# Scores of a sparse-attention step: heads in pairs, the query's high part with the key's low part as two products of 64 rows

## The chip, the cores and the metric

The kernel runs on one core of a Trainium2 chip. The metric is the device time of one execution in microseconds (us), lower is better; the profile and the times below are of the kernel before the change.

## What is computed

One inference step of a decoder of two layers. The first mixes tokens by sparse attention: an indexer scores every key for every query, the best keys are selected, and attention runs over those. The second uses a gated convolution; both have a gated MLP. There are 1024 new prompt tokens and 8 x 4 sample tokens. Cut to the parts that the change touches:

```python
def indexer_scores(qi, wi, ki):
    s = jnp.einsum('bqhd,bsd->bqhs', qi, ki, preferred_element_type=jnp.float32)
    return jnp.einsum('bqhs,bqh->bqs', jax.nn.relu(s), wi.astype(jnp.float32))
...
    s = jnp.einsum('bqkgd,bqjkd->bqkgj', qg, k_sel, preferred_element_type=jnp.float32) * (HEAD_DIM ** -0.5)
    s = jnp.where(valid[:, :, None, None, :], s, -jnp.inf)
    p = jax.nn.softmax(s, axis=-1).astype(v_sel.dtype)
```

Both have 16 heads of 64 dimensions; in the attention four heads share one key head. Prompt queries are worked on in blocks of 128.

## The kernel before

Every fp32 operand of a product is split into a high part (rounded to the matrix format) and a low part (the rest), and a product is built from the products of these parts. `split` (L125) does this: ScalarE copies the high part, VectorE or GpSimd subtracts.

A head has 64 dimensions and TensorE takes 128 rows, so in the scores both parts of a query stand in one stationary tile: the high part in rows 0 to 63 and the low part in rows 64 to 127. The keys' high part stands twice, in both halves of the rows of one tile, and the keys' low part twice in another. So two products of 128 rows, with the high and then with the low keys, add up all four combinations in one PSUM bank. There are three places:

- `index_tile` (L254) makes the indexer queries of block t: `stacks` (L195) writes both parts of each head side by side and `transposed` (L201) turns them into the tile `QI`. For blocks 2 and 3 it goes on to the scores (L278, L279), a relu on ScalarE (L281) and a weighted sum over the heads on VectorE (L285). Blocks 4 to 7 store `QI`.
- `late_scores` (L290) does the scores of blocks 4 to 7 later (L306 holds both products, then L307 and L311), in chunks of up to 512 columns.
- `attend` (L525) does the attention scores of four heads per key head and block (L553, L554). The tile `Q` holds the high part of all rows from ScalarE (L544); GpSimd then subtracts in rows 64 to 127 (L545). VectorE adds the selection bias and takes the maximum while it reads the bank (L555). Then come the exponential (L561), the division on GpSimd (L564), transposes (L570) and the product with the values (L574).

The banks of these products come from the pool tile `ix`: four of them while the index tiles run, two later. The rows of `late_scores` come from a pool tile `e` with 8 buffers.

The other work on TensorE is three products per weight tile in `product` (L711; L719, L720, L722) for the projections behind the attention, the convolution and the MLP, and the input projections (L172 to L174). Scores, selection and attention run as background: generators that `weave` advances between pieces of the foreground, each `yield` with the cost that it stands for. That sets the order in which the program is written; a scheduler that simulates a timeline then sets each engine's own order, and each engine works through its queue in that order.

The sample tokens have products with few rows elsewhere: L629 and L630 (32 rows), L360 (64) and the transposes L689 (64 rows, 64 columns); the change leaves them as they are.

Of the kernel before, what the change touches and what calls it, by code (L numbers as in the profile page):

```python
# [4 lines left out]
F32 = mybir.dt.float32  # L5
# [4 lines left out]
AF = mybir.ActivationFunctionType  # L10
OP = mybir.AluOpType
# [5 lines left out]
NEG = -1e30  # L17
# [54 lines left out]
RL = 4  # L72
R2, D0 = 0.5, 0
F0, R0, R1, C1, C2 = 14, 0.8, 1.0, 115, 70
class Net:
# [119 lines left out]
    def stacks(self, x, rows, n):  # L195

        s = self.p1.tile([128, 16, 128], F32R, name="sq", bufs=1)
        self.split(s[:rows, :n, 0:64], s[:rows, :n, 64:128], x, pool=True)
        return s

    def transposed(self, out, s, n):  # L201
# [52 lines left out]
    def index_tile(self, t, w, q=None):  # L254
        nc = self.nc
        rows = 128 if t < 8 else 32
        if q is None:
            q = self.project(t, w)
        pk = self.new_keys(t, q, q[:rows, 0:WI0].rearrange("p (h d) -> p h d", d=64))
        wi = self.wi[t] if t in self.wi else self.p1.tile([128, 16], F32, name="wi", bufs=2)  # L260
        nc.vector.tensor_scalar(wi[:rows], q[:rows, WI0:WIDX], 1.0 / 32.0, None, op0=OP.mult)
        if t == 8:
            self.index_sample(q, wi, pk)
            return
        s = self.stacks(q[:, 0:1024].rearrange("p (h d) -> p h d", d=64), 128, 16)
        QI = self.p1.tile([128, 16, 128], F32R, name="QI", bufs=2)
        self.transposed(QI, s, 16)
        if t > 3:
            nc.sync.dma_start(self.dQI[t - 4], QI.bitcast(F32))
            self.weave(13.0)  # L270
            return
        n = 128 * (t + 1)
        sc = self.sc[t]
        for h in range(16):
            for c in range(0, n, 512):
                m = min(512, n - c)
                p = self.psx.tile([128, 512], F32, name="ix", bufs=self.nix)[:, :m]
                nc.tensor.matmul(p, QI[:, h, :], self.KIh[:, c:c + m], start=True, stop=False)  # L278
                nc.tensor.matmul(p, QI[:, h, :], self.KIl[:, c:c + m], start=False, stop=True)  # L279
                r = self.p1.tile([128, 512], F32, name="rl", bufs=RL)[:, :m]  # L280
                nc.scalar.activation(r, p, AF.Relu)  # L281
                if h == 0:
                    nc.vector.tensor_scalar(sc[:, c:c + m], r, wi[:, 0:1], None, op0=OP.mult)
                else:
                    nc.vector.scalar_tensor_tensor(sc[:, c:c + m], r, wi[:, h:h + 1], sc[:, c:c + m],  # L285
                                                   op0=OP.mult, op1=OP.add)
            self.weave(n / 512.0)
        nc.vector.tensor_add(sc[:, n - 128:n], sc[:, n - 128:n], self.tri)

    def late_scores(self, blocks, T, K):  # L290

        nc = self.nc
        for t in blocks:
            n = 128 * (t + 1)
            sc = self.sc[t] = T("e", [128, 1024], F32)[:, :n]
            wi = self.wi[t]
            for h in range(16):
                if h % 8 == 0:
                    Q = T("e", [128, 8, 128], F32R)
                    nc.sync.dma_start(Q.bitcast(F32), self.dQI[t - 4][:, h:h + 8])  # L300
                r = T("e", [128, 1024], F32)[:, :n]
                for c in range(0, n, 512):
                    m = min(512, n - c)
                    p = self.psx.tile([128, 512], F32, name="ix", bufs=self.nix)[:, :m]
                    for z in range(2):
                        nc.tensor.matmul(p, Q[:, h % 8, :], K[z][:, c:c + m], start=(z == 0), stop=(z == 1))  # L306
                    nc.scalar.activation(r[:, c:c + m], p, AF.Relu)  # L307
                if h == 0:
                    nc.vector.tensor_scalar(sc, r, wi[:, 0:1], None, op0=OP.mult)
                else:  # L310
                    nc.vector.scalar_tensor_tensor(sc, r, wi[:, h:h + 1], sc, op0=OP.mult, op1=OP.add)  # L311
                yield n / 960.0 + 0.15
            nc.vector.tensor_add(sc[:, n - 128:n], sc[:, n - 128:n], self.trib)

    def index_sample(self, q, wi, pk):
# [209 lines left out]
    def attend(self, g, T, blocks, vs=range(4)):  # L525

        nc = self.nc
        N = 128 * (max(blocks) + 1)
        for v in vs:
            kr = T("r", [128, N], F32)  # L530
            KH, KL = T("KH", [128, N], F32R), T("KL", [128, N], F32R)
            for z in range(2):
                nc.sync.dma_start(kr[64 * z:64 * z + 64], self.dK[v // 2, 64 * (v % 2):64 * (v % 2) + 64, 0:N])
            self.split(KH, KL, kr, pool=True)
            vr = T("qr", [128, N // 128, 64], F32)
            V = T("V", [128, N // 128, 128], F32R)
            nc.sync.dma_start(vr, self.dV[v, :, 0:N // 128])
            self.split(V[:, :, 0:64], V[:, :, 64:128], vr, pool=True)
            for i in blocks:
                n = 128 * (i + 1)  # L540
                qr, Q = T("qr", [128, 4, 128], F32), T("Q", [128, 4, 128], F32R)
                for z in range(2):
                    nc.sync.dma_start(qr[64 * z:64 * z + 64], self.dQ[i][:, 4 * v:4 * v + 4])
                nc.scalar.activation(Q, qr, AF.Copy)  # L544
                nc.gpsimd.tensor_sub(Q[64:128], qr[64:128], Q[64:128].bitcast(F32))  # L545
                st = self.pf.tile([128, 4, 4], F32, name="ast", bufs=2)
                es = []
                for j in range(4):
                    e = T("e", [128, N], F32)
                    for z, c in enumerate(range(0, n, 512)):  # L550
                        m = min(512, n - c)
                        p = self.psx.tile([128, 512], F32, name="ix", bufs=self.nix)[:, :m]
                        nc.tensor.matmul(p, Q[:, j], KH[:, c:c + m], start=True, stop=False)  # L553
                        nc.tensor.matmul(p, Q[:, j], KL[:, c:c + m], start=False, stop=True)  # L554
                        nc.vector.tensor_tensor_reduce(  # L555
                            e[:, c:c + m], p, self.bias[i][:, c:c + m], scale=1.0, scalar=NEG, op0=OP.add,
                            op1=OP.max, accum_out=st[:, j, z:z + 1])
                    if n > 512:
                        nc.vector.tensor_max(st[:, j, 0:1], st[:, j, 0:1], st[:, j, 1:2])
                    nc.vector.tensor_scalar(st[:, j, 1:2], st[:, j, 0:1], -0.125, None, op0=OP.mult)  # L560
                    nc.scalar.activation(e[:, :n], e[:, :n], AF.Exp, bias=st[:, j, 1:2], scale=0.125,  # L561
                                         accum_out=st[:, j, 2:3])
                    nc.vector.reciprocal(st[:, j, 3:4], st[:, j, 2:3])  # L563
                    nc.gpsimd.tensor_scalar(e[:, :n], e[:, :n], st[:, j, 3:4], 1.0, op0=OP.mult, op1=OP.mult)  # L564
                    es.append(e)
                o = self.psv.tile([128, 512], F32, name="pv", bufs=NPV)
                for c in range(i + 1):
                    p = self.tr()
                    for j in range(4):
                        nc.tensor.transpose(p[:, 128 * j:128 * j + 128], es[j][:, 128 * c:128 * c + 128], self.ident)  # L570
                    pp = T("pp", [128, 2, 512], F32R)
                    self.split(pp[:, 0], pp[:, 1], p)
                    for z in range(2):
                        nc.tensor.matmul(o, V[:, c], pp[:, z], start=(c == 0 and z == 0), stop=(c == i and z == 1))  # L574
                ot = T("ot", [64, 512], F32)
                nc.scalar.activation(ot, o[64:128], AF.Copy)
                u = T("ou", [128, 2, 128], F32)
                pick = lambda x, par: x.rearrange("p (c e q) -> p e c q", e=2, q=128)[:, par]
                for par in range(2):
                    nc.vector.tensor_add(u[64 * par:64 * par + 64], pick(ot, par), pick(o[0:64], par))  # L580
                c = g.cols(i)
                nc.sync.dma_start(self.do[g.name][:, 2 * v:2 * v + 2, c:c + 128], u)
                yield n / 100.0 + 2.0
# [874 lines left out]
```

## Time and profile before

| what | value |
|---|---|
| median of 3 runs | 2837.78 us (2833.9 to 2841.37) |
| profiled execution, its own time | 2835.95 us |
| its span | 2834.1 us |
| mean granted TensorE clock | 0.971 of 2.4 GHz |
| TensorE busy | 96% of the span, 15999 products |
| VectorE, ScalarE, GpSimd busy | 64%, 46%, 24% |
| chain of waits by engine | TensorE 74%, VectorE 11%, ScalarE 5%, issue 4%, DMA 4%, GpSimd 2% |

How to read it: a row's busy time is a sum over the whole span, while the kernel has stages with different limits; the index tiles run from some 59 us, the first attention from 250, the late scores from 404 to 684, the second attention from 684 to 1020 and from 1143 to 1340 us with the sample tokens between, and from 1500 us on there are weight products alone. The chain of waits is followed back from the last instruction: at each step to what released it, or to the instruction before it on its engine. Ends of products on TensorE are modelled and overlap the next product; their starts are measured, so the step from start to start is the price of a product in a stream.

### The profile page before, as it was taken

The page shows a single profiled execution, that of the slowest core. Times are in us where ns is not written, and L with a number is a line of the kernel's source. Part 1 is how long each engine was busy: PE and PEld are TensorE (multiplying, and loading weights), DVE is VectorE, ACT ScalarE, POOL GpSimd, SP SyncE. Part 2 cuts the span into 40 slices and gives each one's busy share as a digit, 9 for nine tenths or more (in the row PEclk, how much of TensorE's full clock was granted, in tenths as well). Part 3 has the DMA queues.
Part 4 walks back from the last instruction along what each step waited for, and adds up shares of the span by engine and source line. Part 5 has one row for each costly group of instructions (what it writes and reads, how often), then busy time and mean ns, then how long its engine had stood idle before and what let it go on. Part 6 is the DMA issues. An engine that isn't in the chain of part 4 may idle for free.

```text
span 2834.1 us, 43012 instructions
## 1 busy us (share of the span) xinstructions
PE 2707.1 (96%) x15999; PEld 2379.6 (84%) x15999; DVE 1813.9 (64%) x3348; ACT 1317.1 (46%) x2263; POOL 693.1 (24%) x1026
## 2 busy tenths in 40 slices
PE   7989989899999989997999999999999999999997
PEld 7878757688777868875888999999789987999996
DVE  4474566998889855677686454445754566754446
ACT  4574674765886553356353332323422234432323
POOL 4364641211122354124350000001300031200001
PEclk8989999799999979999999999999999999999999
DMA  4145435133233324331523332323332322332332
GB/s 142 37 165 140 139 104 161 45 90 98 70 91 88 93 82 134 103 91 32 151 78 93 90 90 90 86 80 115 88 91 72 101 80 74 120 90 86 90 92 73
DMA packets 141713, 271.50 MB, mean 96 GB/s; under 512 B 27457, under 2 KB 68865, under 8 KB 140865
## 3 DMA queue, kind: packets, MB, share of 16 engines
q1 hardware_dynamic: 138816, 259.32, 30.8%
q0 software_dynamic: 2688, 9.44, 1.1%
q8 instruction: 126, 2.06, 0.3%
q14 instruction: 83, 0.67, 0.1%
HBM read 245.34 MB, written 23.36 MB: 95 GB/s over the span
## 4 chain that ended last, share of the span: by engine, by line
PE 74%; DVE 11%; ACT 5%; issue 4%; DMA 4%; POOL 2%; SPq 0%; DVEq 0%; ACTq 0%; POOLq 0%
PE mm L722 16%; PE mm L719 16%; PE mm L720 16%; PE m L719 4%; PE m L722 4%; PE m L720 4%; PE pj L172 2%; PE pj L174 2%; PE pj L173 2%; DVE wl L129 2%; PE pv L574 1%; ACT tkb L409 1%; DVE pp L129 1%; PE ix L306 1%; PE tr L570 1%
## 5 line engine op out<-in xcount | busy, mean ns | idle before, releaser
L128 ACT ACTIVATE wh<-raw 128x1024 fp32r<-128x1024 f32 (+2 forms) x456 | 384.3, 843 | 785.4 <-PE mm L720 620.0
L129 DVE TENSOR_TENSOR wl<-raw,wh 128x1024 fp32r<-128x1024 f32 (+2 forms) x456 | 468.1, 1027 | 290.7 <-ACT wh L128 286.3
L719 PE MATMUL mm<-xhB,wh 128*128 128x272 f32 x1920 | 518.4, 289 | 0.0
L720 PE MATMUL mm<-xlB,wh 128*128 128x272 f32 x1920 | 516.6, 287 | 0.0
L722 PE MATMUL mm<-xhB,wl 128*128 128x272 f32 x1920 | 396.6, 288 | 0.6 <-DVE wl L129 0.6
L719 PEld LDWEIGHTS mm<-xhB,wh 128*128 128x128 f32 x1920 | 361.9, 189 | 0.3
L720 PEld LDWEIGHTS mm<-xlB,wh 128*128 128x128 f32 x1920 | 360.8, 188 | 0.3
L722 PEld LDWEIGHTS mm<-xhB,wl 128*128 128x128 f32 x1920 | 299.7, 188 | 0.9 <-DVE wl L129 0.9
L719 PE MATMUL mm<-hh,wh 128*128 128x272 f32 (+1 forms) x992 | 293.7, 311 | 6.0 <-DVE r L760 2.3
L720 PE MATMUL mm<-hl,wh 128*128 128x272 f32 (+1 forms) x992 | 292.5, 310 | 1.9 <-DVE hl L129 1.9
L719 PE MATMUL m<-xhA,wh 128*128 128x512 f32 x608 | 243.0, 401 | 4.9 <-DVE h L844 2.4
L722 PE MATMUL mm<-hh,wl 128*128 128x272 f32 (+1 forms) x992 | 243.9, 311 | 2.2 <-DVE wl L129 2.2
L720 PE MATMUL m<-xlA,wh 128*128 128x512 f32 x608 | 241.6, 397 | 3.0 <-DVE xlA L129 3.0
L722 PE MATMUL m<-xhA,wl 128*128 128x512 f32 x608 | 241.3, 397 | 1.2 <-DVE wl L129 1.0
L719 PEld LDWEIGHTS mm<-hh,wh 128*128 128x128 f32 x992 | 186.5, 188 | 17.9 <-ACT wh L128 4.2
L720 PEld LDWEIGHTS mm<-hl,wh 128*128 128x128 f32 x992 | 186.7, 188 | 11.0 <-DVE hl L129 2.7
L821 POOL COPY ffn_outs<-ext 128x2 f32<-128x2 f32 x44 | 25.8, 586 | 605.9 <-ACT ext L890 605.9
L722 PEld LDWEIGHTS mm<-hh,wl 128*128 128x128 f32 x992 | 161.9, 188 | 12.1 <-DVE wl L129 3.2
L760 DVE TENSOR_TENSOR r<-r,mm 128x544 f32<-128x544 f32 (+1 forms) x128 | 90.5, 708 | 122.6 <-PE mm L722 122.1
L129 DVE TENSOR_TENSOR pp<-tr,pp 128x512 fp32r<-128x512 f32 x168 | 117.7, 713 | 53.6 <-ACT pp L128 53.2
L172 PE MATMUL pj<-W,X 128*128 128x512 f32 (+2 forms) x352 | 133.9, 384 | 16.8 <-ACT W L128 13.3
L564 POOL TENSOR_SCALAR e<-e,ast 128x128 f32<-128x128 f32 (+7 forms) x128 | 101.7, 800 | 194.0 <-DVE ast L563 156.7
(370 smaller groups left out, 5896.8 us busy)
## 6 DMA issues: line engine op xcount, KB each, us to landing
raw<-w_up SPq DMA_DIRECT2D x176, 512.0 KB, 3.5
raw<-w_down SPq DMA_DIRECT2D x128, 256.0 KB, 2.7
raw<-w_ci SPq DMA_DIRECT2D x48, 512.0 KB, 3.6
X<-xp SPq DMA_DIRECT2D x24, 512.0 KB, 3.6
raw<-w_down SPq DMA_DIRECT2D x64, 192.0 KB, 2.4
qr<-dQ SPq DMA_DIRECT2D x64, 128.0 KB, 3.0
raw<-w_ao SPq DMA_DIRECT2D x16, 512.0 KB, 3.5
raw<-w_co SPq DMA_DIRECT2D x32, 256.0 KB, 2.6
```

What stands on the lines that cost most here:

```text
L128: nc.scalar.activation(hi, src, AF.Copy)
L129: (nc.gpsimd if pool else nc.vector).tensor_sub(lo, src, hi.bitcast(F32))
L172: nc.tensor.matmul(p, xh[:, k, :], wh[k][:, s], start=(k == 0), stop=False)
L173: nc.tensor.matmul(p, xh[:, k, :], wl[k][:, s], start=False, stop=False)
L174: nc.tensor.matmul(p, xl[:, k, :], wh[k][:, s], start=False, stop=(k == 7))
L306: nc.tensor.matmul(p, Q[:, h % 8, :], K[z][:, c:c + m], start=(z == 0), stop=(z == 1))
L409: nc.scalar.activation(signs[:r, :n], xs[i], AF.Sign, bias=thr[:r, i:i + 1], scale=-1.0, accum_out=cnt[:r, i:i + 1])
L564: nc.gpsimd.tensor_scalar(e[:, :n], e[:, :n], st[:, j, 3:4], 1.0, op0=OP.mult, op1=OP.mult)
L719: nc.tensor.matmul(o, wh[:, k, :], xh[:, c:c + m], start=(k == 0), stop=False)
L720: nc.tensor.matmul(o, wh[:, k, :], xl[:, c:c + m], start=False, stop=False)
L722: nc.tensor.matmul(o, wl[:, k, :], xh[:, c:c + m], start=False, stop=(k == n - 1))
L760: nc.vector.tensor_add(rv, rv, acc)
```

## The change

The heads are taken in pairs. In the stationary tile the even head keeps its high part in rows 0 to 63, and the odd head has it in rows 64 to 127 (and its low part in rows 0 to 63). The products with the high keys keep 128 rows. The product with the low keys takes the 64 rows of the query's high part alone: rows 0 to 63 for the even head, 64 to 127 for the odd one. The product of both low parts is left out. A new function `qk` issues the four products of a pair: high, high, low, low.

```diff
     def stacks(self, x, rows, n):
         s = self.p1.tile([128, 16, 128], F32R, name="sq", bufs=1)
-        self.split(s[:rows, :n, 0:64], s[:rows, :n, 64:128], x, pool=True)
+        four = s[:rows, :n].rearrange("p (i e) (z d) -> p i (e z) d", e=2, z=2)
+        self.split(four[:, :, 0::3], four[:, :, 1:3], x.rearrange("p (i e) d -> p i e d", e=2), pool=True)
...
+    def qk(self, ps, Q, hi, lo):
+        mm = self.nc.tensor.matmul
+        for p, q in zip(ps, Q):
+            mm(p, q, hi, start=True, stop=False)
+        for z, (p, q) in enumerate(zip(ps, Q)):
+            s = slice(64 * z, 64 * z + 64)
+            mm(p, q[s], lo[s], start=False, stop=True)
...
     def late_scores(self, blocks, T, K):
...
-                r = T("e", [128, 1024], F32)[:, :n]
+                rs = [T("e", [128, 1024], F32)[:, :n] for e in range(2)]
                 for c in range(0, n, 512):
                     m = min(512, n - c)
-                    p = self.psx.tile([128, 512], F32, name="ix", bufs=self.nix)[:, :m]
-                    for z in range(2):
-                        nc.tensor.matmul(p, Q[:, h % 8, :], K[z][:, c:c + m], start=(z == 0), stop=(z == 1))
-                    nc.scalar.activation(r[:, c:c + m], p, AF.Relu)
...
+                    ps = [self.psx.tile([128, 512], F32, name="ix", bufs=self.nix)[:, :m] for e in range(2)]
+                    self.qk(ps, (Q[:, h0 % 8, :], Q[:, h0 % 8 + 1, :]), K[0][:, c:c + m], K[1][:, c:c + m])
+                    for r, p in zip(rs, ps):
+                        nc.scalar.activation(r[:, c:c + m], p, AF.Relu)
...
-                yield n / 960.0 + 0.15
+                yield n / 480.0 + 0.3
...
     def attend(self, g, T, blocks, vs=range(4)):
...
-                nc.gpsimd.tensor_sub(Q[64:128], qr[64:128], Q[64:128].bitcast(F32))
+                for z in range(2):
+                    lo = lambda x: x[64 - 64 * z:128 - 64 * z].rearrange("p (i e) q -> p i e q", e=2)[:, :, z]
+                    nc.gpsimd.tensor_sub(lo(Q), lo(qr), lo(Q).bitcast(F32))
...
-                        nc.tensor.matmul(p, Q[:, j], KH[:, c:c + m], start=True, stop=False)
-                        nc.tensor.matmul(p, Q[:, j], KL[:, c:c + m], start=False, stop=True)
...
+                        self.qk(ps, (Q[:, j], Q[:, j + 1]), KH[:, c:c + m], KL[:, c:c + m])
```

`index_tile` calls `qk` in the same way. In `attend` the pair's two rows are reduced right behind `qk`, and the steps from the maximum on (L558 to L564) are written behind all four heads.

The built program has 352 products of 64 rows (L296 in the changed code; L293 are those with the high keys). Where they stand in TensorE's queue, in the late scores (`ix` the bank, `KH` and `KL` the high and low keys, `e_4835` and `e_4851` the queries), is shown first of before and then of the change:

```order
L306 MATMUL ix_4882<-KH_4446,e_4835 128x512
L306 MATMUL ix_4882<-KL_4447,e_4835 128x512
L306 MATMUL ix_4886<-KH_4446,e_4835 128x256
L306 MATMUL ix_4886<-KL_4447,e_4835 128x256
L306 MATMUL ix_4892<-KH_4446,e_4835 128x512
L306 MATMUL ix_4892<-KL_4447,e_4835 128x512
L306 MATMUL ix_4896<-KH_4446,e_4835 128x256
L306 MATMUL ix_4896<-KL_4447,e_4835 128x256
```

```order
L293 MATMUL ix_4909<-KH_4462,e_4851 128x512
L296 MATMUL ix_4909<-KL_4463,e_4851 128x512
L293 MATMUL ix_4910<-KH_4462,e_4851 128x512
L296 MATMUL ix_4910<-KL_4463,e_4851 128x512
L293 MATMUL ix_4917<-KH_4462,e_4851 128x256
L296 MATMUL ix_4917<-KL_4463,e_4851 128x256
L293 MATMUL ix_4918<-KH_4462,e_4851 128x256
L296 MATMUL ix_4918<-KL_4463,e_4851 128x256
```

The two heads of a chunk now follow each other where a head's two chunks did, but high and low alternate as before: the order high, high, low, low in which `qk` is written isn't kept here. At 28 places it is, as at this one between weight products of the MLP (`m1`), again in the late scores and on TensorE:

```order
L732 MATMUL m1_5080<-xlA_4428,wh_5082 128x512
L293 MATMUL ix_4855<-KH_4462,e_4851 128x512
L293 MATMUL ix_4856<-KH_4462,e_4851 128x512
L296 MATMUL ix_4855<-KL_4463,e_4851 128x512
L296 MATMUL ix_4856<-KL_4463,e_4851 128x512
L734 MATMUL m1_5080<-xhA_4427,wl_5083 128x512
```

Here the two low products stand next to each other. In the second attention, on TensorE between transposes (`tr`) and products with the values (`pv`), they stand apart:

```order
L582 MATMUL tr_11112<-ident_154,e_11014 128x128
L293 MATMUL ix_11288<-KH_11248,Q_11260 128x512
L296 MATMUL ix_11288<-KL_11249,Q_11260 128x512
L586 MATMUL pv_11051<-pp_11107,V_10558 128x512
L293 MATMUL ix_11295<-KH_11248,Q_11260 128x384
L296 MATMUL ix_11295<-KL_11249,Q_11260 128x384
L586 MATMUL pv_11051<-pp_11107,V_10558 128x512
```

A single low product stands between products of 128 rows, as in 296 of the 324 places in all; the place of the scores among the other work has hardly moved.

## Rows read from the trace of the kernel before

**Rows 1.** Busy table of the page: us, share, instructions.

```profile
PE 2707.1 (96%) x15999; PEld 2379.6 (84%) x15999; DVE 1813.9 (64%) x3348; ACT 1317.1 (46%) x2263; POOL 693.1 (24%) x1026
```

**Rows 2.** Windows by stage: stretch, length, busy by engine, granted clock, DMA share, GB/s.

```profile
59.00:146.00 87.00, 85.45 (x497) 72.48 (x496) 44.66 (x54) 52.06 (x104) 27.42 (x31) 1.00 0.12 37
250.00:404.00 154.00, 143.86 (x726) 112.53 (x724) 85.00 (x321) 100.73 (x239) 92.97 (x155) 0.99 0.46 130
404.00:700.00 296.00, 273.81 (x1165) 219.46 (x1166) 251.60 (x433) 179.56 (x324) 50.00 (x73) 0.93 0.31 94
700.00:1020.00 320.00, 302.84 (x1395) 243.60 (x1393) 273.89 (x623) 232.50 (x392) 88.61 (x127) 0.96 0.31 91
1143.00:1340.00 197.00, 181.32 (x861) 142.84 (x860) 141.15 (x361) 103.31 (x176) 60.26 (x57) 0.97 0.27 78
1500.00:2834.00 1334.00, 1307.33 (x9306) 1245.18 (x9304) 738.32 (x1106) 430.44 (x664) 161.41 (x288) 1.00 0.30 90
```

**Rows 3.** Chain of waits by line in 59:146, 404:700, 560:690 and 1143:1340, in turn.

```profile
by line: PE pj L172 15.8%; PE pj L174 15.4%; PE pj L173 15.2%; PE ix L360 9.1%; DVE sc L285 7.6%; PE ix L278 5.1%; PE ix L354 4.6%; PE ix L279 4.3%; PE tr L346 4.0%; ACT rl L281 3.7%; issue 3.5%; DVE sc L288 2.7%; PE tr L207 2.6%; PE tr L32
...
by line: PE m L719 17.1%; PE m L722 17.0%; PE m L720 16.9%; PE ix L306 10.5%; issue 5.7%; DVE e L311 4.6%; DMA h<-doA 2.6%; DMA raw<-w_ao 2.0%; DVE r L981 1.6%; DVE xlA L129 1.6%; ACT tkb L409 1.6%; DMA e<-dQI 1.5%; DVE wl L129 1.5%; DVE tk
...
by line: PE m L722 27.8%; PE m L719 27.7%; PE m L720 27.7%; PE ix L306 15.2%; DVE tkb L400 1.4%; issue 0.5%; DVE r L760 0.0%
...
by line: PE m L720 15.2%; PE m L722 15.1%; PE m L719 15.0%; PE pv L574 7.7%; DVE e L555 7.4%; PE tr L570 6.7%; DVE pp L129 6.2%; PE ix L554 4.8%; PE ix L553 4.5%; DMA r<-dK 4.1%; DVE ast L559 2.4%; issue 2.0%; DVE ou L580 1.6%; ACT e L561 0
```

**Rows 4.** Groups of tile ix, low products: ns min/median/max, first and last start, forms.

```profile
L554 PE MATMUL ix<-KL,Q x192: 221/391/775, 251.1 to 1335.2; 128*128 128x512 f32 x96, 128*128 128x128 f32 x32, 128*128 128x256 f32 x32, 128*128 128x384 f32 x32
L306 PE MATMUL ix<-KL,e x128: 272/394/628, 404.6 to 682.4; 128*128 128x512 f32 x80, 128*128 128x128 f32 x16, 128*128 128x256 f32 x16, 128*128 128x384 f32 x16
L279 PE MATMUL ix<-KI,QI x32: 331/365/399, 59.9 to 142.2; 128*128 128x384 f32 x16, 128*128 128x512 f32 x16
```

**Rows 5.** Timeline of TensorE, 985.9 to 987.3: start, us, line, rows*columns of weights, output.

```profile
985.95 0.40 PE L720 MATMUL m<-hl,wh 128*128 128x512 f32 x1
986.28 0.50 PE L629 MATMUL ix<-bias,selr 32*128 32x512 f32 x1
986.62 0.17 PE L630 MATMUL ix<-bias,selr 32*128 32x32 f32 x1
986.72 0.50 PE L722 MATMUL m<-hh,wl 128*128 128x512 f32 x1
987.06 0.39 PE L719 MATMUL m<-hh,wh 128*128 128x512 f32 x1
987.29 0.39 PE L720 MATMUL m<-hl,wh 128*128 128x512 f32 x1
```

**Rows 6.** The same view, 1089.8 to 1091.4, around a transpose of 64 rows.

```profile
1090.43 0.40 PE L722 MATMUL m<-xhA,wl 128*128 128x512 f32 x1
1090.76 0.27 PE L689 MATMUL pv<-ident,qr 64*128 64x64 f32 x1
1090.96 0.50 PE L719 MATMUL m<-xhA,wh 128*128 128x512 f32 x1
1091.30 0.40 PE L720 MATMUL m<-xlA,wh 128*128 128x512 f32 x1
```

**Rows 7.** The same view, 577.6 to 578.1: score products of 512 and 384 columns.

```profile
577.62 0.40 PE L306 MATMUL ix<-KL,e 128*128 128x512 f32 x1
577.85 0.34 PE L306 MATMUL ix<-KH,e 128*128 128x384 f32 x1
578.03 0.34 PE L306 MATMUL ix<-KL,e 128*128 128x384 f32 x1
```

**Rows 8.** TensorE's waits, 404:700, then 1143:1340: us in total, times, longest.

```profile
PE ix L306 <- ACT e L307: 10.8, 10, 4.3
...
PE ix L553 <- DVE ast L555: 4.3, 3, 1.6
```

**Rows 9.** Costliest group on GpSimd: busy us, mean ns, idle before.

```profile
L545 POOL TENSOR_TENSOR Q<-qr,Q 64x512 fp32r<-64x512 f32 x32 | 41.4, 1295 | 27.9 <-ACT Q L544 22.1 <-issue 3.3 <-POOL KL L129 0.7
```

More of the change, by code (lines that the diff above doesn't have):

```diff
@@ L273, in index_tile @@
         sc = self.sc[t]
-        for h in range(16):
-            for c in range(0, n, 512):
-                m = min(512, n - c)
-                p = self.psx.tile([128, 512], F32, name="ix", bufs=self.nix)[:, :m]
-                nc.tensor.matmul(p, QI[:, h, :], self.KIh[:, c:c + m], start=True, stop=False)
-                nc.tensor.matmul(p, QI[:, h, :], self.KIl[:, c:c + m], start=False, stop=True)
-                r = self.p1.tile([128, 512], F32, name="rl", bufs=RL)[:, :m]
+        for h0 in range(0, 16, 2):
+            ps = [self.psx.tile([128, 512], F32, name="ix", bufs=self.nix)[:, :n] for e in range(2)]
+            self.qk(ps, (QI[:, h0, :], QI[:, h0 + 1, :]), self.KIh[:, :n], self.KIl[:, :n])
+            for h, p in enumerate(ps, h0):
+                r = self.p1.tile([128, 512], F32, name="rl", bufs=RL)[:, :n]
                 nc.scalar.activation(r, p, AF.Relu)
                 if h == 0:
-                    nc.vector.tensor_scalar(sc[:, c:c + m], r, wi[:, 0:1], None, op0=OP.mult)
+                    nc.vector.tensor_scalar(sc[:, :n], r, wi[:, 0:1], None, op0=OP.mult)
                 else:
-                    nc.vector.scalar_tensor_tensor(sc[:, c:c + m], r, wi[:, h:h + 1], sc[:, c:c + m],
-                                                   op0=OP.mult, op1=OP.add)
-            self.weave(n / 512.0)
+                    nc.vector.scalar_tensor_tensor(sc[:, :n], r, wi[:, h:h + 1], sc[:, :n], op0=OP.mult, op1=OP.add)
+            self.weave(n / 256.0)
         nc.vector.tensor_add(sc[:, n - 128:n], sc[:, n - 128:n], self.tri)
+    def qk(self, ps, Q, hi, lo):
[5 more added lines that the diff above has]
+            mm(p, q[s], lo[s], start=False, stop=True)
     def late_scores(self, blocks, T, K):
@@ L296, in late_scores @@
             wi = self.wi[t]
-            for h in range(16):
-                if h % 8 == 0:
+            for h0 in range(0, 16, 2):
+                if h0 % 8 == 0:
                     Q = T("e", [128, 8, 128], F32R)
-                    nc.sync.dma_start(Q.bitcast(F32), self.dQI[t - 4][:, h:h + 8])
-                r = T("e", [128, 1024], F32)[:, :n]
+                    nc.sync.dma_start(Q.bitcast(F32), self.dQI[t - 4][:, h0:h0 + 8])
+                rs = [T("e", [128, 1024], F32)[:, :n] for e in range(2)]
                 for c in range(0, n, 512):
                     m = min(512, n - c)
-                    p = self.psx.tile([128, 512], F32, name="ix", bufs=self.nix)[:, :m]
-                    for z in range(2):
-                        nc.tensor.matmul(p, Q[:, h % 8, :], K[z][:, c:c + m], start=(z == 0), stop=(z == 1))
-                    nc.scalar.activation(r[:, c:c + m], p, AF.Relu)
[L308 to L311, printed above, removed]
-                yield n / 960.0 + 0.15
+                    ps = [self.psx.tile([128, 512], F32, name="ix", bufs=self.nix)[:, :m] for e in range(2)]
+                    self.qk(ps, (Q[:, h0 % 8, :], Q[:, h0 % 8 + 1, :]), K[0][:, c:c + m], K[1][:, c:c + m])
+                    for r, p in zip(rs, ps):
+                        nc.scalar.activation(r[:, c:c + m], p, AF.Relu)
+                for h, r in enumerate(rs, h0):
+                    if h == 0:
+                        nc.vector.tensor_scalar(sc, r, wi[:, 0:1], None, op0=OP.mult)
+                    else:
+                        nc.vector.scalar_tensor_tensor(sc, r, wi[:, h:h + 1], sc, op0=OP.mult, op1=OP.add)
+                yield n / 480.0 + 0.3
             nc.vector.tensor_add(sc[:, n - 128:n], sc[:, n - 128:n], self.trib)
@@ L544, in attend @@
                 nc.scalar.activation(Q, qr, AF.Copy)
-                nc.gpsimd.tensor_sub(Q[64:128], qr[64:128], Q[64:128].bitcast(F32))
+                for z in range(2):
+                    lo = lambda x: x[64 - 64 * z:128 - 64 * z].rearrange("p (i e) q -> p i e q", e=2)[:, :, z]
+                    nc.gpsimd.tensor_sub(lo(Q), lo(qr), lo(Q).bitcast(F32))
                 st = self.pf.tile([128, 4, 4], F32, name="ast", bufs=2)
                 es = []
-                for j in range(4):
-                    e = T("e", [128, N], F32)
+                for j in range(0, 4, 2):
+                    two = [T("e", [128, N], F32) for e in range(2)]
                     for z, c in enumerate(range(0, n, 512)):
                         m = min(512, n - c)
-                        p = self.psx.tile([128, 512], F32, name="ix", bufs=self.nix)[:, :m]
-                        nc.tensor.matmul(p, Q[:, j], KH[:, c:c + m], start=True, stop=False)
-                        nc.tensor.matmul(p, Q[:, j], KL[:, c:c + m], start=False, stop=True)
-                        nc.vector.tensor_tensor_reduce(
-                            e[:, c:c + m], p, self.bias[i][:, c:c + m], scale=1.0, scalar=NEG, op0=OP.add,
-                            op1=OP.max, accum_out=st[:, j, z:z + 1])
+                        ps = [self.psx.tile([128, 512], F32, name="ix", bufs=self.nix)[:, :m] for e in range(2)]
+                        self.qk(ps, (Q[:, j], Q[:, j + 1]), KH[:, c:c + m], KL[:, c:c + m])
+                        for k, (e, p) in enumerate(zip(two, ps), j):
+                            nc.vector.tensor_tensor_reduce(
+                                e[:, c:c + m], p, self.bias[i][:, c:c + m], scale=1.0, scalar=NEG, op0=OP.add,
+                                op1=OP.max, accum_out=st[:, k, z:z + 1])
+                    es.extend(two)
+                for j, e in enumerate(es):
                     if n > 512:
@@ L564, in attend @@
                     nc.gpsimd.tensor_scalar(e[:, :n], e[:, :n], st[:, j, 3:4], 1.0, op0=OP.mult, op1=OP.mult)
-                    es.append(e)
                 o = self.psv.tile([128, 512], F32, name="pv", bufs=NPV)
```

## Prediction

> **What bounds the kernel now.** I read five views. The busy table comes first: TensorE is busy 2707 of 2834 us [rows 1], but its ends are modelled, so that alone settles nothing. The windows, cut by stage, come second [rows 2]: the reader is to see that from 1500 us on TensorE leaves 27 of 1334 us free, and that the change touches nothing there. All score products lie in the five earlier windows, where TensorE leaves 1.5, 10, 22, 17 and 16 us free, 67 us together, while VectorE is almost as busy as TensorE from 404 to 1020 us. The chain of waits comes third [rows 3]: in the two stretches 59 to 146 and 404 to 700 us its largest entries are TensorE's, in 560 to 690 us the three weight products and L306 alone fill 98%, and in 1143 to 1340 us it is mixed with VectorE and DMA. So in these stages TensorE is the bound for about half of the time, and near it for the rest. The groups of the tile `ix` [rows 4] count the products, and the timeline of TensorE [rows 5 to 7] gives the price of one.
>
> **What is removed.** Nothing in number: the 352 products with the low part (192, 128 and 32, [rows 4]) stay 352, each with its own weight load, and only contract over 64 rows instead of 128. A product's step (start to next start) follows its columns: 0.23 us for 512 and 0.18 for 384 [rows 7], so 0.05 per 128 columns and, by that line, an estimate of 0.13 for 256 and 0.08 for 128. By the forms of [rows 4], with the index tiles, there are 192, 64, 48 and 48 low products of these widths: 44.2 + 11.5 + 6.2 + 3.8 = 66 us, and 131 us with the high products. If the two low products of every pair ran at the same time in the two halves, 33 us of TensorE time would go. That needs them next to each other in TensorE's queue. The order of the changed program says they mostly are not: of 324 places with low products only 28 hold two in a row, 296 hold one alone between products of 128 rows, since the scheduler put each low product behind its own high product again.
>
> **What is added: changes of the row count.** The trace of before has such changes elsewhere. At 985.95 us [rows 5] a product of 128 rows and 512 columns is followed by one of 32 rows, and its step is 0.33 us, not the 0.23 of 987.06 to 987.29: 0.10 more. The first product of 128 rows behind the visit takes 0.34: 0.11 more. A product of 64 rows between such neighbours [rows 6] shows the same 0.33 ahead and 0.34 behind, and takes 0.20 us itself with only 64 columns. For 512 columns I add 448 columns at 0.05 per 128, which makes 0.38 against 0.23: 0.15 more. One lone visit thus costs 0.10 + 0.15 + 0.11 = **0.36 us**, nearly whatever its width, as load and pause do not shrink with it. Ends: the wide visit of [rows 5] takes 0.34 itself, with no change of rows right behind it (0.11 more, 0.32 in all); with a pause of 0.10 added to that it would be 0.42. I take 0.36, from the row with 64 rows, the nearest.
>
> A place with two low products has the same 0.21 around it. No row shows two halves of the rows side by side. If they overlap fully the two take 0.38 instead of 0.46: 0.13 more in all; if one follows the other, 0.38 + 0.23: 0.36 more. I take the middle, 0.25. The Trainium skill, page "TensorEngine Tiling (Array Packing)", Key Properties, says that a change of tiling mode drains the engine while a change between tiles of one mode does not, and that tiles work at the same time; by it a pair would cost the lower 0.13, and the sum would be 3 us less.
>
> Sum on TensorE: 296 x 0.36 + 28 x 0.25 = 107 + 7 = **114 us added**; with the ends 296 x 0.32 + 28 x 0.13 = 98 and 296 x 0.42 + 28 x 0.36 = 134.
>
> **How much of it reaches the end.** The score products' share of the chain [rows 3] is 9.4% of 87 us (L278 and L279), 10.5% of 296 (L306) and 9.3% of 197 (L553 and L554): 8.2 + 31.1 + 18.3 = 58 of their 131 us, so 44%. A product on the chain that gets longer moves the end by as much: at least 0.44 x 114 = 50 us. The free time gives the same floor: if all 67 free microseconds took up a delay, 47 would be left. Above, the most is all 114. Much of the free time is waiting for VectorE and ScalarE, whose own inputs come from the delayed products, so I let 40% of what lies between come through: 50 + 0.4 x 64 = 76 us. The end sections from 1500 us on begin that much later and keep their length.
>
> **The rest of the change.** GpSimd's subtraction L545, 32 times 1.30 us [rows 9], becomes two of half the columns. If each took as long as the whole, 41 us more would stand on GpSimd, 21 of them in 250 to 404 us, where it is busy 93 of 154 us [rows 2]; I cost it at nothing, covered by that idle time, since the second subtraction holds up only the odd heads. If the cover were gone, 1.3 us per block, 41 us in all, would be the bound; nearer is its half, some 0.1 us of start-up each, and nothing on the path. The copy and subtraction of the stacks write the same elements in another order: nothing. Activations, the 512-column reductions and the row sums keep their number and widths. In pairs, the second high product waits for the second bank ahead of the first low product; behind it on TensorE's queue are weight products. Waits of that kind are 10.8 us (L306 for L307's activations) and 4.3 us (L553 for L555) now [rows 8]. Where the two stand alone as high, low, high, low, this wait is as before, so I cost it at nothing, between 15 us less and 15 us more.
>
> **Sum.** The profiled execution took 2835.95 us (2834.1 span and 1.85 around it), 1.8 below the median of the three runs. 2836 + 76 = 2912, and 1.8 for the median: **2914 us**, 2.7% slower.
>
> **Rivals.**
> *Row changes cost next to nothing for these products, and the pairs gain* (faster). Place: the pairs in 404 to 700 and 1143 to 1340 us. The pauses of [rows 5, 6] belong to short products with other operands and to transposes; if a 64-row product of a long run did not pause, the 28 pairs would save 28 x 0.19 (66 us over 352) = 5 us, and taking both banks together might shed the waits of [rows 8], 10.8 + 4.3 = 15 us, and some of the rest: 2836 - 20 to 24, about 2814. It decides if a visit costs under some 0.06 us (20 over 324 visits) instead of 0.36. Against it: 32 and 64 rows show the same two pauses at each side. Chance 0.03. The Trainium skill, page "TensorE: Matmul & The Clock Gate", Part 3, says that products in different row groups run at the same time with starts some 4 ns apart; by that rule, were all 176 pairs adjacent, TensorE would shed the 33 us. The rule would need the neighbours that the order does not give, and no run here shows it.
>
> *All of it is absorbed* (no change). The visits cost 114 us, but what follows waits for VectorE anyway: it is busy 252 of 296 us and 274 of 320 [rows 2]. Then 2836, within 8 us. For it: low products early in a stage could use free time later in it. Against it: 67 us free is less than 114, and 560 to 690 us has none [rows 3]. Chance 0.05.
>
> *The visits also cost clock* (slower still). The granted clock in 404 to 700 and 700 to 1020 us is 0.93 and 0.96 of 2.4 GHz [rows 2], so it stood at 1.2 GHz for 14% and 8% of these stretches. More pauses could double that: 0.07 x 296 + 0.04 x 320 = 34 us of engine time, about 2948. Against it: a pause of 0.1 us is short beside the free stretches that stand there today. Chance 0.10; most of it lies in the range.
>
> **How the numbers follow.** The forecast has the remaining 0.82. A measurement of this kernel can tell 0.3%, some 8.5 us, from no change. The floor of the cheap visit, 0.44 x 98 = 43 us, less 15 us of shed waits, gives 2866 with the median; all of 114 us and a third of the clock's 34 gives 2964. Range **2862 to 2962**. Faster 0.03, within 0.3% 0.05, slower 0.92.
>
> **What would show it.** In the timeline after, a high product ahead of a lone low one steps 0.33 us at 512 columns, the low one 0.38, the next product 0.34; between two lone low ones a high product takes about 0.44. The form of the low products reads 64 rows, 352 times. The low line's share of the chain rises over that of the high line. TensorE's windows grow in 404 to 700 us above all, by some 40 us of work, and from the layer's last part on the length is as before. The forecast is wrong if the low products step at 0.23 (price wrong), if the steps are as said but the stages end when they did (absorption), or if the granted clock in the five stretches falls.

## The result, and the profile after

| | time, us (median) | against before |
|---|---|---|
| before | 2836.89 (4 runs) | |
| changed | 2944.59 (2936.27 to 2946.86, 4 runs) | 1.0373, 95% interval 1.0348 to 1.0398 |

The change makes the kernel 108 us slower. The forecast was 2914 us with a range of 2862 to 2962. The profiled execution has a span of 2943.5 us and a mean granted clock of 0.959 (0.971 before).

The busy table of the changed kernel, and its windows, cut where its stages now lie: the index scores, the first attention, the late scores, the second attention ahead of and behind the sample tokens, and the last part (columns as in [rows 2]).

```profile
PE 2836.6 (96%) x15999; PEld 2393.6 (81%) x15999; DVE 1805.4 (61%) x3348; ACT 1323.6 (45%) x2263; POOL 695.3 (24%) x1058
```

```profile
62.00:160.00 98.00, 97.09 (x486) 73.00 (x486) 43.16 (x56) 52.40 (x103) 26.68 (x31) 0.97 0.10 31
263.00:434.00 171.00, 166.65 (x729) 119.05 (x727) 89.28 (x322) 102.33 (x242) 94.08 (x171) 0.94 0.43 117
434.00:740.00 306.00, 302.18 (x1088) 205.06 (x1087) 239.31 (x398) 173.08 (x308) 45.92 (x70) 0.91 0.28 84
740.00:1080.00 340.00, 326.44 (x1445) 248.96 (x1443) 271.36 (x647) 236.41 (x399) 81.69 (x122) 0.99 0.30 89
1208.00:1445.00 237.00, 226.59 (x935) 159.38 (x934) 149.41 (x369) 107.58 (x179) 62.15 (x66) 0.91 0.25 73
...
1609.00:2943.00 1334.00, 1306.99 (x9307) 1245.43 (x9305) 738.76 (x1106) 430.38 (x664) 162.16 (x288) 1.00 0.31 90
```

The number of products is the same 15999, but TensorE is busy 130 us longer; its weight loads differ by 14 us and no other engine by more than 9. Against [rows 2], the last part, cut to the same 1334 us, holds the same work (9307 products against 9306, TensorE busy 1307 us in both). The five windows with score products, 1054 us before, now last 1152: 98 us more; the other 11 us of the span lie in the stretches between them. TensorE's busy time in them grew from 987 to 1119, by 132 us, and its free time fell from 67 to 33 us. So the loss is TensorE time, and about a quarter of it went into time that stood free. The granted clock is lower in four of the five windows (1.00, 0.99, 0.93, 0.96 and 0.97 before; 0.97, 0.94, 0.91, 0.99 and 0.91 after), so some of the added busy time may be products at 1.2 GHz; how much is taken up at the end with the rivals.

The groups of the low products, to be read against [rows 4] (first and last start stand after the durations):

```profile
L296 PE MATMUL ix<-KL,Q x192: 322/491/793, 264.1 to 1440.9; 64*128 64x512 f32 x96, 64*128 64x128 f32 x32, 64*128 64x256 f32 x32, 64*128 64x384 f32 x32
L296 PE MATMUL ix<-KL,e x128: 323/497/794, 434.6 to 735.3; 64*128 64x512 f32 x80, 64*128 64x128 f32 x16, 64*128 64x256 f32 x16, 64*128 64x384 f32 x16
L296 PE MATMUL ix<-KI,QI x32: 435/492/687, 62.6 to 156.6; 64*128 64x384 f32 x16, 64*128 64x512 f32 x16
```

All 352 take 64 rows (64\*128), and the median is 491 to 497 ns where it was 365 to 394. The timeline of TensorE shows what one costs. This is a lone low product of the late scores in the changed kernel, products first and then the weight loads of the same moment (start, us, line, rows\*columns of the weights, output, idle time ahead):

```profile
622.28 0.40 PE L732 MATMUL m<-xlA,wh 128*128 128x512 f32 x1
622.52 0.40 PE L293 MATMUL ix<-KH,e 128*128 128x512 f32 x1
622.85 0.50 PE L296 MATMUL ix<-KL,e 64*128 64x512 f32 x1
623.28 0.50 PE L293 MATMUL ix<-KH,e 128*128 128x512 f32 x1
623.61 0.39 PE L734 MATMUL m<-xhA,wl 128*128 128x512 f32 x1
623.84 0.39 PE L731 MATMUL m<-xhA,wh 128*128 128x512 f32 x1
```

```profile
622.29 0.19 PEld L293 LDWEIGHTS ix<-KH,e 128*128 128x128 f32 x1
622.85 0.18 PEld L296 LDWEIGHTS ix<-KL,e 64*128 64x128 f32 x1 [0.37 <-issue]
623.27 0.19 PEld L293 LDWEIGHTS ix<-KH,e 128*128 128x128 f32 x1 [0.25 <-ACT wh L128]
```

The high product ahead steps 0.33 us, the low one 0.43, the next 0.33, then 0.23 again. In the stream a weight load starts one product early, as the one at 622.29 for the product of 622.52. At both changes of the row count it starts together with its own product, after a pause, so the load is no longer covered by the product ahead.

At the places with two low products in a row (the timeline merges them as x2) the two together take what one alone takes, 511.75 to 512.18:

```profile
511.19 0.63 PE L293 MATMUL ix<-KH,e 128*128 128x512 f32 x2
511.75 0.50 PE L296 MATMUL ix<-KL,e 64*128 64x512 f32 x2
512.18 0.50 PE L731 MATMUL m<-xhA,wh 128*128 128x512 f32 x1
512.52 0.39 PE L732 MATMUL m<-xlA,wh 128*128 128x512 f32 x1
```

The second low product starts 3 or 4 ns behind the first. So the two halves do work side by side, but there are only 28 such places.

From these steps the prices for the experiments follow. A lone low product costs, at 512 columns, 0.10 ahead + 0.20 itself (0.43 against 0.23) + 0.10 to 0.11 behind, 0.40 us; at 128 columns it steps 0.25 where the 128-row product of that width steps 0.11 (e1's trace), 0.35 in all. Two in a row cost 0.10 + (0.43 - 0.46) + 0.11 = 0.18. On TensorE that makes 296 x 0.40 + 28 x 0.18 = 123 us, some 2 us less with those of 128 columns at 0.35.

### The profile page after: what moved, and what is told of

It reads as the page before. It is cut to its first block, busy times and chain, and to the rows that moved or that the text cites. A ratio compares the mean times of both kernels' runs of the same rounds, so it can differ in the third digit from the quotient of the medians.

```text
span 2943.5 us, 43081 instructions
## 1 busy us (share of the span) xinstructions
PE 2836.6 (96%) x15999; PEld 2393.6 (81%) x15999; DVE 1805.4 (61%) x3348; ACT 1323.6 (45%) x2263; POOL 695.3 (24%) x1058
## 5 line engine op out<-in xcount | busy, mean ns | idle before, releaser
L128 ACT ACTIVATE pp<-tr 128x512 fp32r<-128x512 f32 x168 | 101.9, 635 | 110.4 <-PE tr L582 67.1
```

Source lines behind the costliest of these rows:

```text
L128: nc.scalar.activation(hi, src, AF.Copy)
```

## The experiments

Each line is against the kernel before on the same chip. The part of an edit is a difference of two ratios times 2837 us; by the intervals it is good to some 6 to 9 us. The forecasts of e2 to e4 started from 2837 us, without the 11 us that e1 then showed for the pairs, so these three are read against e1.

| kernel | median, us | ratio, 95% interval |
|---|---|---|
| e1, low products of 128 rows | 2848.84 | 1.0038 (1.0025 to 1.0052) |
| e2, high, high, low, low forced | 2879.66 | 1.0144 (1.0127 to 1.0161) |
| e3, 64 rows in the late scores alone | 2884.48 | 1.0160 (1.0143 to 1.0177) |
| e4, in the second attention alone | 2884.26 | 1.0155 (1.0137 to 1.0172) |
| e5, in the first attention alone | 2863.72 | 1.0089 (1.0062 to 1.0117) |
| e6, as e1, softmax behind each pair | 2847.96 | 1.0034 (1.0022 to 1.0047) |
| e7, kernel before, low products in rows 0 to 63 | 2952.30 | 1.0396 (1.0373 to 1.0418) |
| e8, as e2, both low products in rows 0 to 63 | 2913.69 | 1.0265 (1.0245 to 1.0285) |
| e9, as e1, attention as before | 2844.31 | 1.0020 (1.0009 to 1.0031) |
| e10, index tiles alone, four heads at once | 2855.88 | 1.0069 (1.0043 to 1.0096) |

**Is it the row count (e1)?** In `qk`, nothing else:

```diff
-            s = slice(64 * z, 64 * z + 64)
+            s = slice(0, 128)
```

> The changed kernel with the low products over all 128 rows again (so both low parts are multiplied too, as before the change); pairs, layout and the order of every queue stay as in the changed kernel. Theory P (the changes of the row count are the whole loss): back to the time of before, 2837 us, within 8 us. Rival Q (the pairs, their banks and the coarser pieces of background cost a part): it keeps 20 us or more of the 108, so 2857 or over. Rival F (the pairs by themselves gain): under 2828.

Measured: 1.0038. So 1.0373 - 1.0038 = 95 us hang on the row count and 11 us on the pairs; theory P holds for nine tenths, and the rest is more than its 8 us. In the two traces TensorE works through the same 15999 products in the same order, so the rows of the low products are the only difference there. Compared product by product, the two profiled executions differ by 98 us (2943.5 against 2845.7): the steps of the 763 products at visits (the low ones and the neighbour on each side) that ran at the full granted clock in both are 77 us longer, those of the 141 that ran at 1.2 GHz in one or both 28 us longer, and all other products together are 6 us shorter. The groups of the low products in this kernel:

```profile
L296 PE MATMUL ix<-KL,Q x192: 272/388/628, 251.1 to 1343.4; 128*128 128x512 f32 x96, 128*128 128x128 f32 x32, 128*128 128x256 f32 x32, 128*128 128x384 f32 x32
L296 PE MATMUL ix<-KL,e x128: 273/395/628, 405.3 to 673.7; 128*128 128x512 f32 x80, 128*128 128x128 f32 x16, 128*128 128x256 f32 x16, 128*128 128x384 f32 x16
L296 PE MATMUL ix<-KI,QI x32: 331/366/400, 60.1 to 142.4; 128*128 128x384 f32 x16, 128*128 128x512 f32 x16
```

Durations are those of [rows 4] again. The late scores end 9 us earlier than before (673.7 against 682.4), the attention ends 8 us later (1343.4 against 1335.2): in pairs the scores gain a little and the second attention loses more.

**Which stage (e3, e4, e5)?** `qk` gets a flag, and only one caller passes 64 rows:

```diff
-            s = slice(64 * z, 64 * z + 64)
+            s = slice(64 * z, 64 * z + 64) if half else slice(0, 128)
```

> Low products of 64 rows in late_scores alone (118 places with one, 5 with two), 128 rows in the index tiles and both attentions; all queues in the order of the changed kernel. 118 x 0.40 + 5 x 0.18 = 48 us of TensorE time. Theory P with the mean share of 87%: 2837 + 42 = 2879 us. Rival A (part of it is absorbed where VectorE is almost as busy; in the changed kernel the stretch of the late scores grew by 23 us only): 2837 + 23 = 2860 us.

> Low products of 64 rows in the second attention alone (98 places with one, 15 with two), 128 rows elsewhere; all queues in the order of the changed kernel. 98 x 0.40 + 15 x 0.18 = 42 us of TensorE time. Theory P with 87%: 2837 + 37 = 2874 us. Rival C (the pauses also cost granted clock here: the changed kernel's stretch from the end of the late scores to the end of this attention grew by 53 us, and its granted clock fell from 0.97 to 0.91 at the end): 2837 + 53 = 2890 us.

> Low products of 64 rows in the first attention alone (54 places with one, 5 with two), 128 rows elsewhere; all queues in the order of the changed kernel. 54 x 0.40 + 5 x 0.18 = 22 us of TensorE time. The kernel with 128 rows everywhere takes 2849 us. Theory P with 80% at the end: 2867 us. Rival A (absorbed, since the chain of waits in 250 to 404 us before the change names DMA and ScalarE nearly as often as TensorE): 2855 us or less.

Against e1, the late scores cost 35 us (1.0160 - 1.0038) of the 48 priced on TensorE, the second attention 33 of 42 and the first 14 of 22. The late scores lie between theory P (42) and rival A (23), nearer to P. The rest of the 95 us, 13, is left for the index tiles, priced at 11; they were not run alone with 64 rows in this form, but between e1 and the changed kernel the stretch from their first to their last low product grows from 82 to 94 us, and that of the late scores from 268 to 301. The first attention lies nearer to theory P (18) than to rival A (6), within some 9 us. No stage hides its part, and within the noise none costs more than its price. Rival C wanted 53 us in the second attention and fails in that size: the 53 us by which its stretch grew were not this edit's alone. Its reason doesn't fail with it, since the mean granted clock is lower than e1's 0.973 in all three profiled executions (0.965, 0.966 and 0.967).

**Do the neighbours matter (e2, e8)?** In e2 each low product is tied behind the one ahead of it in TensorE's order:

```diff
...
+            self.tc.add_manual_dep(i.ins, last.ins.name, mybir.DependencyInfo(
+                mybir.DependencyClass.NoSync, mybir.DependencyReason.DATA), reason="in order")
+            last = i
```

> The changed kernel with the order high, high, low, low forced on TensorE's queue, so that 173 places hold two low products in a row and 6 hold one, in place of 28 and 296. By the steps that the trace of the changed kernel shows (a lone low product 0.40 us more than a 128-row one with its neighbours, two in a row 0.18 us more) TensorE has 173 x 0.18 + 6 x 0.40 = 34 us added, not 123. Theory P: 87% of that reaches the end, as in the changed kernel, so +29 us: 2866 us, within 12. Rival Q (waiting for both banks at once holds TensorE up): 2890 us or more.

e8 has the same order with `s = slice(0, 64)` for both heads, and the layout of the heads as before the change.

> The kernel with high, high, low, low forced, but both low products of a pair in rows 0 to 63 (layout of the heads as before the change). Theory O (two low products overlap because they use different halves: the trace shows the second starting 0.003 us behind the first): here the second follows by its own 0.23 us at 512 columns, 0.19 on the average, so 173 x 0.19 = 33 us more on TensorE than with both halves, some 28 at the end: 2908 us. Rival N (any two products of 64 rows overlap): 2880 us, as with both halves.

e2 lies 30 us above e1, for 34 us priced and 29 expected: two thirds of the loss go with the lone places. Rival Q, that waiting for both banks holds TensorE up, fails: 2880 us is under its 2890. e8 lies 34 us above e2, for 33 priced. The timelines, of e2 and then of e8, both in the index tiles at 512 columns:

```profile
129.37 0.50 PE L294 MATMUL ix<-KI,QI 64*128 64x512 f32 x2
129.80 0.73 PE L291 MATMUL ix<-KI,QI 128*128 128x512 f32 x2
130.46 0.50 PE L294 MATMUL ix<-KI,QI 64*128 64x512 f32 x2
```

```profile
136.17 0.73 PE L290 MATMUL ix<-KI,QI 128*128 128x512 f32 x2
136.84 0.73 PE L293 MATMUL ix<-KI,QI 64*128 64x512 f32 x2
137.49 0.33 PE L207 MATMUL tr<-ident,sq 128*128 128x128 f32 x1
```

Two low products take 0.43 us with both halves and 0.65 with one (136.84 to 137.49): the 0.22 between them is a whole product, and the two changes of the row count are paid in both. So it is the different halves that overlap, and the change of rows that costs.

**Is the price the visit's alone (e7)?** The kernel before the change, with `Q[:64]` and the first 64 rows of the low keys in its three places; like the changed kernel it leaves out the product of both low parts.

> The kernel before the change with one edit: the low products take rows 0 to 63 alone, for all heads, without pairs and without the odd heads' swapped halves. All 352 stand alone, 352 x 0.40 = 141 us of TensorE time. Theory P (a price per visit, whatever the half, 78% of it at the end as in the changed kernel against the one with 128 rows): +110 us, 2949 us within 12. Rival H (it is the odd heads' half or the pairs that cost): under 2920.

2952 us, by the ratio 112 us above before. In its trace 338 low products stand alone and 7 places hold two in a row, so not quite all 352 are lone and the price is some 138 us: 81% of it came through. Rival H fails. No pairs and no swapped halves are needed for the loss.

**Where do the pairs lose 11 us (e6, e9)?** e6 moves the loop over the maximum, exponential and division (L570 to L577 of the changed kernel) into the loop over pairs. e9 keeps the pairs in `index_tile` and `late_scores` and has `attend` and `stacks` as before.

> The kernel with 128-row low products in pairs, with one edit: in the attention the steps from the maximum to the division stand behind each pair of heads, no longer behind all four. With them behind all four, that kernel was 10 us (0.4%) over the time before, and its trace loses them in the end of the second attention, where little foreground work is left. Theory S (the late softmax is what costs): 2839 us, within 4. Rival G (the pairs' banks and the coarser pieces cost): stays at 2849.

> Pairs with 128-row low products in the index tiles and late_scores alone; the attention and the stacks as before the change. In the kernel with pairs everywhere the late scores ended 9 us earlier than before (674 against 683 us). Theory G1 (that gain stays): 2830 us, faster than both. Rival G2 (it is given back, as the attention waits for the selection on VectorE anyway): 2839 us, within 4.

Neither theory of a gain holds: e6 is at 1.0034, within the interval of e1, so the late softmax is not it; e9 is at 1.0020, so the earlier end of the late scores is given back, as rival G2 has it (its reason wasn't tested), and some 6 of the 11 us come with the pairs in the scores. What carries it stays open. No version here beats the kernel before.

**How many low products per change (e10)?** In the index tiles alone, groups of four heads in four banks, the order forced as in e2, halves in turn; the pieces of background between the groups are twice as long.

> Index tiles alone with low products of 64 rows, in groups of four heads in the forced order high x 4, low x 4 (halves in turn), four banks at once; 128 rows elsewhere. Theory O predicts steps of the four low products of 0.003, 0.23, 0.003 and 0.43 us at 512 columns, with 0.21 for the neighbours 0.88 us against 4 x 0.23 = 0.92: a group of four is where the halves begin to pay. On the time: 2849 us as with 128 rows everywhere, within 4. Rival N (each half pauses for the next product of the same half): a second step of 0.4 us.

```profile
128.18 1.14 PE L291 MATMUL ix<-KI,QI 128*128 128x512 f32 x4
129.25 0.73 PE L294 MATMUL ix<-KI,QI 64*128 64x512 f32 x4
129.92 0.67 PE L208 MATMUL tr<-ident,sq 128*128 128x128 f32 x4
```

The four low products take 0.67 us (129.25 to 129.92), as theory O has it; with some 0.2 for the neighbours 0.87 against 0.92. Only their sum fits: the trace has steps of 0.003, 0.33, 0.006 and 0.32 us, so the second is neither O's 0.23 nor rival N's 0.4, but N's steps with its last of 0.43 would make over 0.8. By the steps, four products per change are about where the halves stop costing. The time doesn't show it: 1.0069 (from 1.0043) is 9 us over e1's 1.0038 where 4 at most were expected. The two intervals overlap, so a loss isn't shown either, and a gain of 0.05 us in each of eight groups could not be seen.

## Why the prediction was right

- **The bound.** As read: where weight products stand alone nothing changed, and 98 us of the loss lie in the five windows, on TensorE. Not in the late scores "above all", though: against e1 they cost 35 us, the second attention 33. The order of the built program, not the text of `qk`, decided it: 296 lone places and 28 pairs, as counted.
- **The price of a visit.** 0.36 us was taken, with ends 0.32 and 0.42; it is 0.40. The neighbours were right (0.10 and 0.11). The low product's own step was taken as 0.38, from a 64-column transpose with columns added; it is 0.43. The pause behind a wide 64-row product is as long as that behind the 128-row one ahead, which was the case of the upper end. A high product between two lone low ones steps 0.43 us, where 0.44 was said.
- **Two in a row.** 0.25 was taken between 0.13 and 0.36; it is 0.18, which is the end where the halves overlap fully, with 0.43 in place of 0.38. The Trainium skill, page "TensorEngine Tiling (Array Packing)", Key Properties, says that a change of tiling mode drains the engine and a change of tile doesn't. The traces agree: 0.33 us ahead of a change, 0.43 for one or for two low products. The Trainium skill, page "TensorE: Matmul & The Clock Gate", Part 3, has products in different row groups start some 4 ns apart; the trace has 3 to 4 ns. Both rules hold here at once, and the first is what the pairs run into.
- **The sum on TensorE.** 114 us was predicted; the measured steps make 123.
- **How much reaches the end.** Two thirds (76 of 114) was predicted; 95 of 123 came through, 77%, together with whatever the lower clock added. The stages alone gave 73% (late scores), 79% (second attention) and 64% (first). If the clock's part is the 22 us estimated below, the steps by themselves brought 73 us, 59%. So it isn't decided whether "I let 40% of what lies between come through" was too little, or whether the forecast lacked a term for the clock. The floor from the chain of waits, 44%, lies below all of these; it counted nothing for the first attention and for 700 to 1020 us. The free time in the five windows fell by 34 us, where the forecast implied 38 of a smaller sum. The rival in which all is absorbed fails.
- **The rest of the change.** It was costed at nothing, between 15 us less and 15 us more; e1 shows 11 us more. GpSimd's part was right: the two subtractions take 0.77 us each where one took 1.30 [rows 9], 7.6 us more in all on an engine that is busy 24% as before; two halves take 0.24 us more than the whole, so the start-up is 0.12 each, where some 0.1 was said.

```profile
L556 POOL TENSOR_TENSOR Q<-qr,Q 64x256 fp32r<-64x256 f32 x64 | 49.0, 766 | 44.6 <-ACT Q L553 19.7 <-issue 15.9 <-DMA raw<-w_down 4.3
```

- **The rivals.** Free changes of the row count: refuted by the steps. The clock: the prediction named a lower granted clock in the five stretches as a sign that it is wrong, and in four of them it is lower. The means, of the changed kernel and then of e1:

```profile
core 0: 2943.5 us, clock 0.959
core 0: 2845.7 us, clock 0.973
```

What is missing to full clock is 0.041 x 2943.5 = 121 us against 0.027 x 2845.7 = 77, so at most 44 us of engine time went that way (the rival put 34 on it). In the runs of the kernel before on e5's chip 0.974 goes with 2831 us and 0.967 with 2843, some 1.7 us per 0.001; the medians of the runs are 0.972 for e1 and 0.959 for the changed kernel, which makes an estimate of 22 us. The 77 us at visits at full clock show that most of the loss needs no clock. So this rival is right in part: the clock fell, by an estimate it carries about a quarter of the 95 us, and whether the pauses brought it down isn't shown.
- **The signs that can't be read.** The chain of waits of the changed kernel isn't followed back past 1460 us, so the share of the low products on it is unknown.

The 31 us between forecast and result are, by these numbers, 11 for the pairs, some 6 for the price (9 us more on TensorE, two thirds of it) and some 13 for the share or the clock (123 us at 77% instead of 67%). All three err to the same side, so the hit does not rest on errors that cancel; it rests on a range wide enough, with the measured time in its upper fifth. The ends of the range don't quite follow from the prediction's sums: it works them out as 2866 and 2964 (2963 when added up) and then takes 2862 and 2962.

## What to carry to other kernels

Contracting over 64 rows saves TensorE time only if two products with different halves stand next to each other in TensorE's own queue, and then, by the steps of one trace, only from about four such products per change of the row count (no version here got faster by it): a lone one among 128-row products cost 0.40 us more than the same product with 128 rows, whose own step is 0.23. Look at the order that the scheduler made, not at the order in which the code issues. For an addition to an engine that is busy 92 to 98% of a stage, the chain's share of the touched products is a floor below what arrives: here 64 to 81% came through, with the lower clock's part in it.

## What the runs showed that was not expected

A weight load of 64 rows isn't started during a product of 128 rows, nor the other way: in the lone visit above the load row stood idle 0.37 us ahead of the low product and 0.25 behind, so a change pays the pause and the load. It is so at every change in the changed kernel's trace: the load starts 1 to 3 ns ahead of its own product at all 340 changes from 128 to 64 rows and at most 31 ns ahead at all 338 changes back, but 124 ns ahead (the median) between products of 128 rows. And a second product of 64 rows in the same half adds only its own step (0.65 us for two, 0.43 for one), so the price is one of the change and not of each 64-row product.
